# A two-layer hybrid decoder step: compression chunks, later modulation and first modulation issued in other portions

## The chip, the cores and the metric

The kernel runs on one core of one Trainium2 chip. Its time is the device time of one execution in microseconds (us), as a median of runs. The engines are named as in the profile: PE is TensorE's matrix array and PEld its weight loads, DVE is VectorE, ACT is ScalarE, POOL is GpSimd, and SP is SyncE, which here issues every DMA, in program order.

## The reference

Two layers of a trunk run over 544 tokens with D_MODEL = 1024: a prompt of 512 tokens, and 8 sequences of 4 sampled tokens with a paged past of 2048 rows each. All in float32. Per layer:

```python
mod = silu(c) @ ada_w + ada_b                 # 9 rows of c (1 prompt, 8 samples), 3072 columns
shift, scale, gate = split(mod, 3)
h = rmsnorm(x, norm_g) * (1 + scale) + shift
proj = h @ w_in                               # u, z_s5, q, k/v, gates, z_nsa, merge logits
y5 = gelu(s5_scan(u)); y5 = y5 * sigmoid(y5 @ glu_w + glu_b) * silu(z_s5)
kc, vc = compress_rows(past and new k/v)      # silu((64 rows * 64 + pe) @ w1) @ w2 per block of 64 rows
o = gated sum of compressed, selected and window attention
out = (sig(m_s5) * (y5 @ w_s5_out) + sig(m_nsa) * ((o * silu(z_nsa)) @ w_nsa_out)) @ w_o
x = x + gate * out
```

A last rmsnorm follows, and the new key/value rows, window rows and S5 states are returned too.

## The kernel before

Activations lie transposed, with features on partitions: eight blocks `k` of 128 features by 544 tokens, the tokens in two halves of 256 and 288 columns. A dense block (`wblk`, 39 per layer) is 128 output features: its 512 KB of weights are loaded, split into a high and a low part on ACT and DVE, and multiplied in 8 k-blocks x 3 matmuls x 2 halves = 48 matmuls of 128x128 weights (function `mm`).

The order of the instructions on each engine is fixed when the program is built. The code is written as threads (Python generators) with priorities, a small number first: `modulation` 4 (first) and 25 (later), `modulate` 3, compression 15, the S5 branch 2 to 6, prompt attention 20, sample attention 5, the dense stream 50. The planner `_Sched` keeps a cost model of PE, the other engines and the DMA queue, and always issues the ready thread of the smallest number; it turns to the dense stream when other work has had PE for FAIR = 12 us, or when its model of PE's load says that the present slice of time has had too few columns (`lags`). So the dense stream is the filler. Threads also wait for events (`ev`, `done`) and for columns of one arena of 49504 columns (`alloc`). Each engine then executes its list strictly in order: a matmul whose data have not landed holds back all matmuls behind it, and a DMA that waits for its buffer holds back SP's later DMAs.

What the change touches:

- `modulation` (L524) computes `mod` and `amul` = (1 + scale) * norm_g. A k-block is one 512 KB load and four matmuls of 32-column weights (`scT`) by 256 columns, side by side in four column strips of the array; they show as eight instructions, since each float32 matmul is run in two passes. Eight k-blocks give one part; per layer there are three parts, of which parts 0 and 1 hold shift and scale for four feature blocks each and part 2 the gate. The first call loads parts 0 and 1 of layer 0 (16 loads at once). The later call (`LATER`, 4 parts, 32 k-blocks) runs from event `h` of layer 0 with one buffer (`ADA_N` = 1): load, wait, four matmuls, next load.
- `modulate` (L620) makes `h`. In layer 0 it scales x by the inverse norm in place, then, for each half of the features, waits for `mod`, forms the high part on ACT, the value on DVE and the low part on DVE; the 32 sample columns go through POOL (`samples`), and their low part is a POOL subtraction (`sample_parts`).
- `first_u` (in `dense`): blocks u0 and u1 are multiplied first. With `EARLY` = 1, u0 takes the first half of the features when that half of `h` is done, and everything else follows the second half.
- `products` multiplies a compression chunk: 64 matmuls of 64-column weights by 64 columns (68 in the first chunk, 20 for the new rows), 128 instructions. It gives way after every `PROD_STEP` = 2 steps, that is after four matmuls. There are 8 chunks of past rows per layer (`compress`) and one of new rows (`compress_new`). A chunk's page rows are 16 loads of 128 KB, into one buffer in layer 0 and two in layer 1.
- `compress(1)` starts after attention of layer 0 (`att`), `s5(l)` after `h`. `ps5` and `tbank` may use PSUM bank 5 once the event `ada` says that the later modulation is done.

Of the kernel before, what the change touches and what calls it, by code (L numbers as in the profile page):

```python
# [11 lines left out]
F32 = mybir.dt.float32  # L12
# [278 lines left out]
def body(ctx: ExitStack, tc: tile.TileContext, A, O):  # L291
# [232 lines left out]
    def modulation(parts, na, pace, banks, between=None):  # L524

        n = 256
        for l, part in parts:
            if part == 0:
                L[l]["mod"] = const.tile([P, 24, 9], F32, name=nm("mod"))
                L[l]["amul"] = const.tile([P, 8, 9], F32, name=nm("amul"))  # L530
# [51 lines left out]
        done("ada", parts)  # L582

# [36 lines left out]
    def modulate(l):  # L620
# [5 lines left out]
        if l == 0:  # L626
            accb = yield from alloc(N)
            for k in range(8):
                square_acc(accb.v(N), xt(k), k)
            w_dma(1)  # L630
# [13 lines left out]
        def tokens(k, a):  # L644
            tk = evr.next().v(256)
            dve.scalar_tensor_tensor(tk, xt(k)[:, a:a + 256], amul[:, k, 0:1], rstd[:, a:a + 256],
                                     op0=ALU.mult, op1=ALU.mult)
            act.activation(hh(k, a, a + 256), tk, AF.Identity, bias=mod[:, k, 0:1])
            prev.append((hl(k, a, a + 256), tk, mod[:, k, 0:1], hh(k, a, a + 256).bitcast(F32)))
# [3 lines left out]
        def samples(ks):  # L653

            sb = [P, 4, NB, TS]
            for k2 in range(ks.start, ks.stop, 2):
                xs = xb[k2 // 2].v(2, N)[:, :, T:N]
                if l:
                    pool.tensor_tensor(ts_[:, k2:k2 + 2], xs, rstd[:, None, T:N].to_broadcast([P, 2, NS]), op=ALU.mult)
                    xs = ts_[:, k2:k2 + 2]  # L660
                xs = xs.rearrange("p k (b t) -> p k b t", t=TS)
# [4 lines left out]
        def sample_parts(ks):  # L666
            for k2 in range(ks.start, ks.stop):
                act.copy(hh(k2, T, N), ts_[:, k2])
                pool.tensor_tensor(hl(k2, T, N), ts_[:, k2], hh(k2, T, N).bitcast(F32), op=ALU.subtract)
        for half in range(2):  # L670
            if l == 0:
                ks = range(4 * half, 4 * half + 4)
                for k in ks:
                    dve.tensor_tensor(xt(k), xt(k), rstd, op=ALU.mult)
                yield t()
                w_hi(half + 1)
                w_lo(half + 1)
                yield ev("mod", l, half)
                mod, amul = q["mod"], q["amul"]
                for k in ks:  # L680
                    x_, tk = xt(k)[:, 0:T], misc.next().v(T)
                    act.activation(hh(k, 0, T), x_, AF.Identity, scale=amul[:, k, 0:1], bias=mod[:, k, 0:1])
                    dve.tensor_scalar(tk, x_, amul[:, k, 0:1], mod[:, k, 0:1], op0=ALU.mult, op1=ALU.add)
                    prev.append((hl(k, 0, T), tk, hh(k, 0, T).bitcast(F32)))
                    if len(prev) > 1:
                        dve.tensor_tensor(*prev.pop(0), op=ALU.subtract)
                dve.tensor_tensor(*prev.pop(0), op=ALU.subtract)
                done("hp", l, half)
                samples(slice(ks.start, ks.stop))
                sample_parts(ks)  # L690
            else:
                for part in range(2):
                    yield ev("mod", l, part)
                yield ev("rstd", l - 1, half)
                mod, amul = q["mod"], q["amul"]
                if half:
                    samples(slice(0, 4))
                    samples(slice(4, 8))
                for k in range(8):
                    tokens(k, 256 * half)  # L700
                    if k % 2:
                        yield t()
                dve.scalar_tensor_tensor(*prev.pop(0), op0=ALU.add, op1=ALU.subtract)
                if half:
                    sample_parts(range(8))
                done("hp", l, half)
# [9 lines left out]
    def dense(l):  # L716
# [51 lines left out]
        def first_u():  # L768
# [5 lines left out]
            if l == 0:  # L774
                outs = [[B[2 * t_ + h][:, 0:HALVES[h][1] - HALVES[h][0]] for h in range(2)] for t_ in range(2)]
                for part in range(2):
                    yield ev("hp", l, part)
                    for t_, h in ((t_, h) for t_ in range(2) for h in range(2)):
                        if t_ < EARLY:
                            yield from mm(w[t_], 0, 8, hh, hl, h, False, outs[t_][h], range(4 * part, 4 * part + 4))  # L780
                        elif part:
                            yield from mm(w[t_], 0, 8, hh, hl, h, False, outs[t_][h])
                        if part:
# [4 lines left out]
                            if t_:  # L788
                                wahead(h)
# [133 lines left out]
        def outputs():  # L923
            q["ogb"] = yield from alloc(4 * N)
# [232 lines left out]
    def ps5(l):  # L1157

        banks = ([7] if ("prs", l) in S.events else [2, 3]) + ([5] if ("ada", LATER) in S.events else [])
# [207 lines left out]
    def s5_tile(l, t_, K):  # L1367
# [8 lines left out]
        db3 = yield from alloc(1224, True)  # L1376
        yield w_
# [246 lines left out]
    def compress_new(l):  # L1624
# [5 lines left out]
        vcbd = q["vcbd"] = q["kcb"].v(8, 64, p=64, at=528)  # L1630
        cwb = []
# [682 lines left out]
```

## Time and profile before

| | |
|---|---|
| device time, median of 3 runs | 1291.28 us (1289.97 to 1294.87) |
| profiled execution: device time | 1290.52 us |
| its span, first to last instruction | 1288.7 us |
| PE / PEld busy | 1180.2 us (92%) / 1057.9 us (82%) |
| DVE / ACT / POOL busy | 781.8 us (61%) / 476.2 us (37%) / 149.2 us (12%) |
| mean granted TensorE clock | 0.959 of 2.4 GHz |
| HBM read, written | 211.84 MB, 37.98 MB |

A clock of 1.0 is 2.4 GHz, 0.5 is 1.2 GHz. The tables by stretch (windows) give the busy time of each engine in that stretch with the number of instructions that touch it, then clock, busy share of the DMA engines and GB/s. All instructions carry line 229, that of the recording helper, so operations are told apart by tile names and shapes: `scT` is modulation, weights 128x64 by 64 columns compression, weights 128x128 by 256 or 288 columns the dense stream.

### The profile page before, as it was taken

What the parts mean: (1) busy time and instruction counts of PE and PEld (TensorE: products, weight loads), DVE (VectorE), ACT (ScalarE), POOL (GpSimd) and SP (SyncE); (2) the same over time, 40 slices, a digit from 0 to 9 for tenths busy, and PEclk for the clock granted to TensorE, in tenths of its full rate; (3) what the DMA queues carried; (4) which work ended last, traced back from release to release, by engine and by line L of the source; (5) the groups of instructions that cost most, each with busy time, mean ns of one, the idle gap of its engine ahead of it and who ended that gap; (6) DMA issues with size and microseconds to landing.
All of it is one profiled execution on the core that took longest, in us unless ns stands there. A gap on an engine that the chain in (4) does not pass through costs nothing.

```text
span 1288.7 us, 30956 instructions
## 1 busy us (share of the span) xinstructions
PE 1180.2 (92%) x11994; PEld 1057.9 (82%) x11994; DVE 781.8 (61%) x1791; ACT 476.2 (37%) x1120; POOL 149.2 (12%) x337
## 2 busy tenths in 40 slices
PE   5699889989999999997998889899999999999995
PEld 2588778889887888887988878789988788789995
DVE  4575676523666676566435377876865667563744
ACT  4332332222445444443224333333444445443321
POOL 0213043100100000000001023240110000000001
PEclk9799998999999999998998999978999999999997
DMA  9576854765765767339785534545466565633742
GB/s 372 194 234 183 251 170 150 229 224 204 246 215 170 231 196 213 95 104 327 234 264 171 181 127 129 175 142 163 144 210 208 179 196 159 197 95 110 263 126 79
DMA packets 178357, 243.54 MB, mean 189 GB/s; under 512 B 33441, under 2 KB 129954, under 8 KB 176930
## 3 DMA queue, kind: packets, MB, share of 16 engines
q1 hardware_dynamic: 178210, 241.56, 59.1%
q8 instruction: 95, 1.56, 0.5%
q14 instruction: 52, 0.43, 0.1%
HBM read 211.84 MB, written 37.98 MB: 194 GB/s over the span
## 4 chain that ended last, share of the span: by engine, by line
PE 61%; DVE 13%; DMA 11%; SPq 5%; ACT 4%; issue 4%; POOL 1%; DVEq 0%; ACTq 0%
PE bank L229 61%; DVE m L229 13%; SPq L229 5%; ACT m L229 4%; DMA m<-in_ada_w 4%; DMA m<-ud 2%; DMA m<-in_cw 1%; DMA kpd<-m 1%; POOL m L229 1%; DMA m<-kpd 1%; DMA c_k<-in_k 1%; ACT L229 0%; DMA m<-in_s5k 0%; SPq L1518 0%; DMA m<-in_cmp 0%
## 5 line engine op out<-in xcount | busy, mean ns | idle before, releaser
L229 PE MATMUL bank<-m,m 128*128 128x288 f32 (+10 forms) x10796 | 1073.2, 281 | 49.3 <-DVE m L229 24.9
L229 PEld LDWEIGHTS bank<-m,m 128*128 128x128 f32 (+4 forms) x10796 | 964.5, 168 | 134.5 <-issue 48.4
L229 DVE TENSOR_TENSOR m<-m,m 128x256 f32<-128x256 f32 (+16 forms) x631 | 389.3, 640 | 175.4 <-ACT m L229 156.3
L229 ACT COPY m<-bank 128x128 f32<-128x128 f32 (+7 forms) x256 | 99.3, 398 | 341.4 <-PE bank L229 323.8
L229 ACT CAST m<-m 128x1024 fp32r<-128x1024 f32 (+6 forms) x274 | 174.5, 650 | 79.7 <-DVE m L229 47.6
L229 PE MATMUL bank<-c_k,m 128*128 128x128 f32 (+1 forms) x562 | 88.6, 285 | 18.8 <-DVE m L229 12.7
L229 ACT ACTIVATE m<-m 128x64 f32<-128x64 f32 (+7 forms) x76 | 35.4, 469 | 172.8 <-DVE m L229 163.1
L229 PEld LDWEIGHTS bank<-c_k,m 128*128 128x128 f32 (+1 forms) x562 | 65.0, 144 | 31.9 <-DVE m L229 16.5
L229 ACT ACTIVATE m<-bank 128x288 f32<-128x288 f32 (+4 forms) x130 | 50.6, 390 | 107.3 <-PE bank L229 106.8
L229 POOL TENSOR_TENSOR m<-m,m 128x32 f32<-128x32 f32 (+4 forms) x104 | 57.2, 571 | 188.8 <-ACT m L229 166.3
L229 DVE TENSOR_REDUCE m<-bank 128x1 f32<-128x384 f32 (+4 forms) x132 | 57.2, 473 | 28.8 <-PE bank L229 28.7
L229 ACT ACTIVATE m<-bank,m 128x384 f32<-128x384 f32 (+4 forms) x132 | 67.9, 524 | 18.0 <-DVE m L229 14.5
L229 POOL CAST m<-m 64x128 fp32r<-64x128 f32 x64 | 22.9, 358 | 424.1 <-ACT m L229 392.0
L229 DVE COPY m<-bank 128x32 f32<-128x32 f32 (+6 forms) x104 | 39.4, 385 | 50.1 <-ACT m L229 31.9
L229 DVE SCALAR_TENSOR_TENSOR m<-m,bank 128x256 f32<-128x256 f32 x96 | 41.3, 431 | 29.0 <-ACT m L229 13.2
L229 PE MATMUL bank<-m,scT 128*32 128x256 f32 x384 | 35.3, 463 | 24.1 <-DMA m<-in_ada_w 24.0
L229 DVE TENSOR_SCALAR m<-m,m,m 128x128 f32<-128x128 f32 (+4 forms) x132 | 52.5, 438 | 2.5
L229 POOL TENSOR_TENSOR m<-m,c_k 128x256 f32<-128x256 f32 (+2 forms) x32 | 31.3, 980 | 177.1 <-PE bank L229 145.7
L229 DVE TENSOR_TENSOR m<-bank,c_k 128x256 f32<-128x256 f32 (+5 forms) x52 | 16.7, 323 | 48.5 <-PE bank L229 47.5
L229 POOL MEMSET m<- 128x32 f32 (+5 forms) x52 | 8.3, 181 | 289.8 <-PE bank L229 149.8
L229 DVE SCALAR_TENSOR_TENSOR m<-m,m 128x64 f32<-128x64 f32 (+5 forms) x64 | 29.6, 487 | 20.1 <-ACT m L229 19.6
L229 PEld LDWEIGHTS bank<-m,scT 128*32 128x32 f32 x384 | 9.9, 123 | 33.7 <-DMA m<-in_ada_w 14.1
(62 smaller groups left out, 411.9 us busy)
## 6 DMA issues: line engine op xcount, KB each, us to landing
m<-in_wblk SPq DMA_DIRECT2D x78, 512.0 KB, 4.3
m<-in_cmp SPq DMA_DIRECT2D x256, 128.0 KB, 3.5
m<-in_kvsel SPq DMA_DIRECT2D x256, 128.0 KB, 3.1
m<-in_ada_w SPq DMA_DIRECT2D x48, 512.0 KB, 5.4
m<-in_cw SPq DMA_DIRECT2D x8, 1024.0 KB, 8.4
m<-in_wo SPq DMA_DIRECT2D x16, 512.0 KB, 3.9
ms<-m SPq DMA_DIRECT2D x16, 272.0 KB, 4.9
m<-ms SPq DMA_DIRECT2D x16, 272.0 KB, 3.7
```

Of the source, the lines that this page charges most:

```text
L229: return f(*args, **kw)
```

## The change

- First modulation in quarters: a new thread `modulation_first` (priority 2) replaces the first call. `ada_q` holds the same weights in quarters of two feature blocks, two loads of 1 MB each, all eight issued at once. A matmul takes 512 columns; the four column strips now hold four different k-blocks of the same 512 outputs, and four matmuls with a constant `fold` add the strips, where two transposes stood.
- `modulate` of layer 0 goes by quarters: per feature block two DVE operations of 512 columns with the inverse norm as an operand (the pass over x in place is gone), ACT between them; the low part of the sample columns moves from POOL to DVE. `first_u` follows in quarters with u0 and u1.
- Later modulation: the rest of layer 0 (8 k-blocks) starts after compression of layer 0, the three parts of layer 1 (24 k-blocks) after attention of layer 0. Two buffers, both k-blocks in one visit, 1.5 us of waiting added in the plan after their loads.
- `PROD_STEP` = 32: a chunk's 64 matmuls are issued in one visit.
- A new event `s5m`: `compress_new(0)` and the buffer for the outputs wait until the fourth S5 tile has its columns. `page_table` and its clamp, and the second pack of constants, are loaded after the first quarter. PSUM bank 5 is free per layer.

```diff
@@ modulation
             w = aw[i % na].v(1024)
-            yield "for", [ps], [w]
+            if i % na == 0:
+                yield "for", [ps], [b.v(1024) for b in aw]
+                yield t(ADA_LATE)
             for j in range(4):
                 pe.matmul(ps[32 * j:32 * j + 32, 0:n], scT[:, k, :], w[:, j * n:(j + 1) * n],
                           start=(k == 0), stop=(k == 7))
-            if i + na < len(todo):
-                load(i + na)
-            else:
-                aw[i % na].free()
+            if i % na == na - 1:
+                for n_ in range(na):
+                    if i + 1 + n_ < len(todo):
+                        load(i + 1 + n_)
+                    else:
+                        aw[n_].free()
@@ new
+    def modulation_first(banks):
...
+        for qd in range(4):
+            for kh in range(2):
+                sp.dma_start(aw[2 * qd + kh].v(2048), A["ada_q"][qd, kh])
+            if qd < 2:
+                w_dma(qd + 1)
+        ae = yield from alloc(512, True)
+        for qd in range(4):
+            ps, e = banks[qd % len(banks)], ae.v(512)
+            for kh in range(2):
+                w = aw[2 * qd + kh].v(4, 512)
+                yield "for", [ps], [w]
+                for j in range(4):
+                    pe.matmul(ps[32 * j:32 * j + 32, :], scT[:, 4 * kh + j, :], w[:, j, :], start=(kh == 0), stop=(kh == 1))
+                aw[2 * qd + kh].free()
+            act.copy(e, ps)
+            yield w_
+            for i in range(4):
+                pe.matmul(ps[:, 16 * i:16 * i + 9], e[:, i * P:(i + 1) * P], C["fold"][:, 0:9], start=True, stop=True)
...
+            done("modq", qd)
@@ modulate, layer 0
+        def tokens(k, a, n=256):
+            tk = misc.next().v(n) if n > 288 else evr.next().v(n)
+            dve.scalar_tensor_tensor(tk, xt(k)[:, a:a + n], amul[:, k, 0:1], rstd[:, a:a + n], op0=ALU.mult, op1=ALU.mult)
+            act.activation(hh(k, a, a + n), tk, AF.Identity, bias=mod[:, k, 0:1])
+            prev.append((hl(k, a, a + n), tk, mod[:, k, 0:1], hh(k, a, a + n).bitcast(F32)))
...
-                pool.tensor_tensor(hl(k2, T, N), ts_[:, k2], hh(k2, T, N).bitcast(F32), op=ALU.subtract)
-        for half in range(2):
-            if l == 0:
-                ks = range(4 * half, 4 * half + 4)
-                for k in ks:
-                    dve.tensor_tensor(xt(k), xt(k), rstd, op=ALU.mult)
...
+                (pool if l else dve).tensor_tensor(hl(k2, T, N), ts_[:, k2], hh(k2, T, N).bitcast(F32), op=ALU.subtract)
+        for qd in range(0 if l else 4):
+            w_hi(min(qd, 1) + 1)
+            w_lo(min(qd, 1) + 1)
+            yield ev("modq", qd)
+            mod, amul = q["mod"], q["amul"]
+            ks = slice(2 * qd, 2 * qd + 2)
+            for k in range(ks.start, ks.stop):
+                tokens(k, 0, T)
+            samples(ks)
+            dve.scalar_tensor_tensor(*prev.pop(0), op0=ALU.add, op1=ALU.subtract)
+            sample_parts(range(ks.start, ks.stop))
+            done("hp", l, qd)
@@ outputs of dense; s5_tile; compress_new
+            yield ev("s5m", l)
+        if t_ == 3:
+            done("s5m", l)
+        if l == 0:
+            yield ev("s5m", l)
@@ main
-            yield ev(*ADA_EV)
-            yield from modulation(LATER, ADA_N, ADA_PACE, [B[5]])
+            for i in range(DEPTH):
+                yield ev(*ADA_EV[i])
+                yield from modulation(LATER[i], ADA_N[i], ADA_PACE, [B[5]])
@@ constants
-LATER = ((0, 2),) + tuple((l, part) for l in range(1, DEPTH) for part in range(3))
-ADA_N = 1
+LATER = ((0, 2),), ((1, 0), (1, 1), (1, 2))
+ADA_N = 2, 2
+ADA_LATE = 1.5
-ADA_EV = 'h', 0
+ADA_EV = ('cmp', 0), ('att', 0)
-PROD_STEP = 2
+PROD_STEP = 32
```

## Rows read from the trace of the kernel before

**Rows 1.** Windows of four stretches: us, busy of each engine, clock, DMA share, GB/s.

```profile
64.00:300.00 236.00, 215.81 (x2495) 194.96 (x2493) 135.71 (x243) 65.81 (x124) 49.16 (x99) 0.96 0.68 214
...
424.00:574.00 150.00, 148.32 (x1484) 129.18 (x1483) 98.45 (x253) 68.63 (x182) 5.60 (x16) 1.00 0.54 164
574.00:604.00 30.00, 22.76 (x163) 21.12 (x162) 19.33 (x40) 10.01 (x22) 0.00 (x0) 0.92 0.85 290
...
578.00:700.00 122.00, 108.39 (x1277) 101.96 (x1276) 62.30 (x144) 36.07 (x65) 0.38 (x4) 0.94 0.80 259
```

**Rows 2.** Waits of PE for modulation weights: us, times, longest.

```profile
PE bank L229 <- DMA m<-in_ada_w: 24.0, 7, 12.4
```

**Rows 3.** Timeline of PE in the opening: start, us, instructions, idle before and releaser.

```profile
36.98 1.57 PE L229 MATMUL bank<-m,m 128*128 128x288 f32 x5 [3.16 <-POOL m L229]
...
41.23 2.27 PE L229 MATMUL bank<-m,scT 128*32 128x256 f32 x24
...
47.53 12.10 PE L229 MATMUL bank<-m,m 128*128 128x256 f32 x71 [0.51 <-DVE m L229]
63.14 0.97 PE L229 MATMUL bank<-m,scT 128*32 128x256 f32 x8 [3.52 <-DMA m<-in_ada_w]
```

**Rows 4.** Timeline of the other engines in the opening.

```profile
23.84 0.40 ACT L229 COPY m<-bank 128x288 f32<-128x288 f32 x1 [3.07 <-PE bank L229]
...
31.63 5.93 POOL L229 TENSOR_TENSOR m<-m,m 128x32 fp32r<-128x32 f32 x4 [1.76 <-ACT m L229]
...
45.34 0.20 DVE L229 SCALAR_TENSOR_TENSOR amul<-mod,c_k 128x36 f32<-128x36 f32 x1
```

**Rows 5.** Windows of two stretches of the opening's transfers.

```profile
0.00:20.00 20.00, 6.70 (x44) 3.68 (x44) 6.75 (x17) 8.49 (x13) 0.21 (x4) 1.00 0.92 349
...
23.00:29.00 6.00, 5.51 (x46) 2.45 (x48) 4.66 (x9) 2.21 (x4) 0.44 (x2) 1.00 1.05 408
```

**Rows 6.** DMA issues: count, KB each, median us from issue to landing.

```profile
m<-in_ada_w SPq DMA_DIRECT2D x48, 512.0 KB, 5.4
...
m<-in_wo SPq DMA_DIRECT2D x16, 512.0 KB, 3.9
...
m<-in_xT SPq DMA_DIRECT2D x4, 544.0 KB, 5.4
```

**Rows 7.** Groups by form: busy us, mean ns of one, of DVE's modulation in layer 1.

```profile
L229 DVE SCALAR_TENSOR_TENSOR m<-m,mod,m 128x256 fp32r<-128x256 f32 x16 | 7.9, 492 | 0.9 <-ACT m L229 0.9
L229 DVE SCALAR_TENSOR_TENSOR m<-m,amul,m 128x256 f32<-128x256 f32 x16 | 7.9, 501 | 5.4 <-ACT m L229 5.4
```

**Rows 8.** Timeline of PE at two later visits of modulation.

```profile
100.26 0.64 PE L229 MATMUL bank<-m,scT 128*32 128x256 f32 x8 [3.21 <-DMA m<-in_ada_w]
...
287.03 0.64 PE L229 MATMUL bank<-m,scT 128*32 128x256 f32 x8 [2.01 <-DMA m<-in_ada_w]
```

**Rows 9.** Windows cut at single visits on PE, start to start of the next.

```profile
73.97:75.54 1.57, 1.57 (x48) 1.50 (x48) 1.57 (x4) 0.46 (x1) 1.57 (x3) 1.00 1.01 313
...
299.26:302.90 3.64, 3.64 (x121) 3.58 (x120) 1.07 (x2) 1.47 (x2) 0.00 (x0) 1.00 0.93 349
272.62:273.00 0.38, 0.38 (x9) 0.31 (x8) 0.00 (x0) 0.00 (x0) 0.00 (x0) 1.00 0.00 0
893.30:894.90 1.60, 1.60 (x50) 1.48 (x48) 1.29 (x3) 0.28 (x1) 0.00 (x0) 1.00 0.12 37
302.90:304.53 1.63, 1.63 (x17) 1.49 (x13) 0.61 (x1) 0.00 (x0) 0.00 (x0) 1.00 0.07 28
...
652.57:661.63 9.06, 9.06 (x76) 8.93 (x72) 5.29 (x13) 3.46 (x5) 0.00 (x0) 1.00 0.81 262
84.59:85.16 0.57, 0.57 (x12) 0.16 (x9) 0.57 (x2) 0.00 (x0) 0.00 (x0) 1.00 0.00 0
```

**Rows 10.** Window of a stretch at the lower clock.

```profile
288.70:291.90 3.20, 3.20 (x16) 3.20 (x15) 0.00 (x0) 0.29 (x1) 0.00 (x0) 0.50 1.02 381
```

**Rows 11.** Timeline of ACT between the layers' attention and projection.

```profile
601.39 1.35 ACT L229 CAST m<-m 128x1024 fp32r<-128x1024 f32 x2 [7.71 <-DMA m<-in_nsaow]
```

More of the change, by code (lines that the diff above doesn't have):

```diff
@@ L527, in modulation @@
         for l, part in parts:
-            if part == 0:
+            if part == 0 and l:
                 L[l]["mod"] = const.tile([P, 24, 9], F32, name=nm("mod"))
@@ L582, in modulation @@
         done("ada", parts)
+    def modulation_first(banks):
+        mod = L[0]["mod"] = const.tile([P, 24, 9], F32, name=nm("mod"))
+        amul = L[0]["amul"] = const.tile([P, 8, 9], F32, name=nm("amul"))
+        aw = []
+        for _ in range(8):
+            aw.append((yield from alloc(2048, True)))
+        for qd in range(4):
[16 more added lines that the diff above has]
+                pe.matmul(ps[:, 16 * i:16 * i + 9], e[:, i * P:(i + 1) * P], C["fold"][:, 0:9], start=True, stop=True)
+            fs = slice(2 * qd, 2 * qd + 2)
+            src = ps[:, 0:64].rearrange("p (s q b) -> p s q b", s=2, q=2)[:, :, :, 0:9]
+            dst = mod[:, 0:16].rearrange("p (s f) b -> p s f b", s=2)[:, :, fs]
+            bia = C["ada_b"][:, 0, 0:16].rearrange("p (s f) -> p s f", s=2)[:, :, fs]
+            dve.tensor_tensor(dst, src, bia[:, :, :, None].to_broadcast([P, 2, 2, 9]), op=ALU.add)
+            dve.scalar_tensor_tensor(amul[:, fs, :], mod[:, 8 + 2 * qd:10 + 2 * qd, :], 1.0,
+                                     C["norm_g"][:, 0, fs, None].to_broadcast([P, 2, 9]), op0=ALU.add, op1=ALU.mult)
+            done("modq", qd)
+            if qd % 2:
+                done("mod", 0, qd // 2)
+            yield t()
+        ae.free()
     def rstd_of(acc, r, h):
@@ L668, in sample_parts @@
                 act.copy(hh(k2, T, N), ts_[:, k2])
-                pool.tensor_tensor(hl(k2, T, N), ts_[:, k2], hh(k2, T, N).bitcast(F32), op=ALU.subtract)
-        for half in range(2):
-            if l == 0:
-                ks = range(4 * half, 4 * half + 4)
-                for k in ks:
-                    dve.tensor_tensor(xt(k), xt(k), rstd, op=ALU.mult)
[L675 to L706, printed above, removed]
@@ new lines, in modulate @@
+        for half in range(2 if l else 0):
+            for part in range(2):
+                yield ev("mod", l, part)
+            yield ev("rstd", l - 1, half)
+            mod, amul = q["mod"], q["amul"]
+            if half:
+                samples(slice(0, 4))
+                samples(slice(4, 8))
+            for k in range(8):
+                tokens(k, 256 * half)
+                if k % 2:
+                    yield t()
+            dve.scalar_tensor_tensor(*prev.pop(0), op0=ALU.add, op1=ALU.subtract)
+            if half:
+                sample_parts(range(8))
+            done("hp", l, half)
@@ L775, in first_u @@
                 outs = [[B[2 * t_ + h][:, 0:HALVES[h][1] - HALVES[h][0]] for h in range(2)] for t_ in range(2)]
-                for part in range(2):
+                for part in range(4):
                     yield ev("hp", l, part)
[L778 to L783, printed above, removed]
+                    for t_, h in ((t_, h) for t_ in range(2) for h in range(2)) if part == 3 else ((t_, h) for h in range(2) for t_ in range(2)):
+                        if t_ and not part:
+                            continue
+                        ks = range(0 if t_ and part == 1 else 2 * part, 2 * part + 2)
+                        yield from mm(w[t_], 0, 8, hh, hl, h, False, outs[t_][h], ks)
+                        if part == 3:
                             flush()
@@ L2196, in _consts @@
     c["dmask"] = (row[:, None] % 16 == np.arange(16)[None, :]).astype(f)
+    c["fold"] = np.tile(np.eye(32, dtype=f), (4, 1))
     c["mvals"] = np.tile(np.arange(9, dtype=f), (P, 1))
```

36 lines of the change are left out of this document (14 added, 22 removed).

## Prediction

> **What bounds the kernel now.** I read the windows by stage first. From 64 to 300 us PE is busy 215.8 of 236 us, from 424 to 574 148.3 of 150, and between the two layers, from 574 to 604, only 22.8 of 30 [rows 1]. The dense stream fills PE under attention, so in these stretches a microsecond of work or of standing still that is taken from PE comes off the end, as long as nothing else becomes late. The second view is the list of waits: PE stood still for modulation weights for 24.0 us in 7 waits, 12.4 of them at the very start, when nothing can run, and 11.6 in six waits later [rows 2]. The third is PE's timeline of the opening, the fourth PE's order of instructions, cut at single visits.
>
> **The opening.** Now: PE has the first matmuls of u0 in its queue, and those that need the sample columns wait for POOL's four subtractions (5.93 us from 31.63) [rows 4]; PE stands 3.16 us at 36.98, and behind it stand the weights of the second half, which are computed only at 41.23 although they have landed [rows 3]. `amul` of that half is done at 45.5 [rows 4], u0 and u1 run from 46.4 to 59.6, then PE waits 3.52 us for the first later k-block, and u2 starts at 64 [rows 3].
>
> After: ahead of the end of the last quarter lie x (4 x 544 KB), modulation (8 MB) and two dense blocks of 512 KB [rows 6], together 11.7 MB. At 349 GB/s for 20 us and 408 after that [rows 5] it has landed at 31.5 us; I take 33 for the constants ahead of it. Behind it: one group of eight instructions of 512 columns, twice the 0.76 us that eight of 256 columns take at the mostly low clock of that place (2.27 us for 24) [rows 3], so 1.5 us; then an eviction, four small matmuls and two small DVE operations, some 2.5 us (an estimate from a 0.40 us eviction and a 0.20 us DVE operation [rows 4], with the waits between). So the last `amul` stands at 37 rather than 45.5. The inverse norm, done at 24.2 now [rows 4], is then no longer what is late. `h` of a quarter takes four DVE operations of 512 columns, each at least 0.5 us and at most twice that [rows 7], 2 to 4 us, with ACT between and the sample columns behind: the last quarter is done at 41 to 42. Its 24 matmuls take 3.0 us at 2.4 GHz (72 take 9.06 [rows 9]), 6 at 1.2. PE may still have a backlog of the 72 matmuls of the earlier quarters. So u2 starts between 45 and 53; I take 50, **-14 us** (-11 to -19). POOL and DVE have less to do here than before, and SP issues the same bytes in fewer DMAs. Moving the page table and the constants behind costs nothing: they are first used after `h`.
>
> **Waits for later weights.** After the opening five waits are left, 11.6 - 3.5 = 8.1 us [rows 2, 3], the largest 3.21 and 2.01 [rows 8]. The k-blocks leave that stretch, so **-8.1 us**; the next instruction in PE's list is dense work whose weights are loaded two blocks ahead, and SP is no longer held by buffers waiting for PE. After three of the waits (at 63, 100 and 287 us) the granted clock reads 0.50 for 3.4 us (one stretch is shown [rows 10]); at that level 3.4 us do the work of 1.7, so **-5.1 us** more. Both could be 0 if other waits take the place.
>
> **Chunks in one visit.** A visit of 8 instructions takes 0.38 us and one of 120 takes 3.64 [rows 9]: 0.029 per instruction and 0.15 to come in. Dense work pays too: 72 matmuls take 9.06 us, so 12 should take 1.51, but 12 behind a visit take 1.63 (and 1.79 elsewhere where all are of 288 columns) [rows 9]; I take 0.15, together 0.30 per visit. I count 60 visits, from 73.97 to 893.4 us (first and last in [rows 9]), over 18 chunks: 42 fewer, 12.6 us. About 20 of the 42 are in the second layer, some of them where PE has room anyway, so **-10 us** (-6 to -13). What waits behind a chunk waits up to 3.9 us (128 instructions): S5 steps, and the dense stream whose weights then are ready. The 120 instructions in a row ran at clock 1.00 [rows 9].
>
> **Two k-blocks in a visit.** 32 visits become 16. A single visit costs 0.57 us [rows 9], a k-block inside a long run 0.76 at a low clock [rows 3], so at full clock between half of that and all of it; what a visit saves is 0.15 of dense work and between -0.2 and 0.2 of its own. 16 of them: **-4 us** (+1 to -5). The PE work itself moves and stays.
>
> **What it costs.** 24 k-blocks, 12.6 MB, move into the stretch from 578 to 700 us, where the DMA engines are busy 0.80 and move 259 GB/s, 31.6 MB in 122 us [rows 1]. The added waits stand in PE's list: each of the 12 visits waits for two loads, and all dense matmuls queue behind it, and SP's loads for the next pair behind the matmuls. No row shows this traffic in this place. Lower bound 0: a load of 512 KB for the same stretch's projection lands in 3.9 us [rows 6], and the plan now adds 1.5 us of waiting. Upper bound: every visit waits as long as the longest later one did, 3.5 us [rows 3], and a low stretch of 1.7 follows it: 62 us. The nearest rows are the later visits before: 11.6 us over the 18 visits up to 287 us, 0.64 each; 12 x 0.64 = **+8 us**. At the turn itself, `nsaow` weights are already late, ACT waits 7.71 us for them [rows 11]; two more loads (1.05 MB at 340 GB/s or so) can go ahead of them: **+3 us**. The layer's `mod` is needed after 8 of the 12 visits; at 8 us for each (two loads, the 1.5 us, a place on PE) they are done 64 us after attention, some 35 us before the next layer's `h`, so that wait I put at 0. Memory: at that turn the buffers of the second modulation (2448 columns) and `h` (8976) don't both fit beside compression by my count, which would hold `h` back until the projection ends, 0 to 8 us; I take 0 since modulation should then be over. `s5m` I put at nothing: before, the fourth S5 tile had its columns long before `compress_new(0)` got its own.
>
> The page "DMA: Bandwidth & Descriptors" of the Trainium skill (Specifications) gives some 358 GB/s as the limit of one core's share of HBM. The trace passes it for a short while with 408 GB/s [rows 5]. By the page the 31.6 + 12.6 MB need at least 123 us, all of a stretch of 122; by the row 108.
>
> **Sum.** -14 - 8.1 - 5.1 - 10 - 4 + 8 + 3 = -30 us. The profiled execution took 1290.5 us (span 1288.7), so 1260; the median of the runs is 0.8 us above that execution: **1261 us**. About 0.5% (6.5 us) is what a measurement of this kernel can tell from no change.
>
> **Rivals.**
> - Part of the gain is handed back between the layers (17%). Loads crowd with page loads, the visits wait 2 us each rather than 0.64: +16, and half of the visits leave a low stretch, +10, less what is counted: -30 + 16 + 10 - 8 + 8 for `h` without columns = -4 to -12: 1279 to 1287. For it: 0.80 and 0.85 DMA shares before anything is added [rows 1]. Against it: projection loads land in 3.9 us there.
> - Slower (8%): the same place, but each of the 12 visits waits 3 us and is followed by a low stretch of 1.7: +56 + 3 - 41 = +18, 1309. It decides from (41 - 3) / 12 = 3.2 us a visit, clock included. For it: single waits of 3.5 and 3.21 have been seen [rows 3, 8]; against it, 12 of those 18 visits did not wait at all.
> - The opening doesn't get shorter (5%): at clock 0.50 the dense quarters queue up to 53 us and something else, such as the third block's weights, keeps u2 at 60: -4 instead of -14, 1271.
> - One-visit chunks lower the clock (2%): 16 chunks x 1.7 us = +27, 1288. The stretch with 120 instructions speaks against it.
> - More gain (8%): no waits at the turn and modulation filling the 7 idle us there, -41 - 7: 1242.
>
> **How the numbers follow.** The forecast, 60%, holds 1245 to 1277. Faster: 60 + 8 + 5 + two thirds of 17 (11) = 84%; within 0.5%: 6 + 2 = 8%; slower: 8%. A range from 1242 to 1285 leaves out about 6 below and 13 above.
>
> **What would show it.** Opening: the first 128x288 dense matmul of u2 near 50 us, the last `amul` near 37. Waits for `in_ada_w`: none between 64 and 300 us, new ones after 578. Compression: 18 visits of 128 instructions of 3.9 us each, and clock 1.00 behind them. Modulation's matmuls in pairs of k-blocks, 16 instructions in about 1 us. If the opening gains under 8 us, or PE's waits between 578 and 700 grow by over 25 us, the prediction is wrong.

## The result, and the profile after

The changed kernel takes **1268.5 us** (median of 4 runs, 1266.2 to 1271.5) against 1291.2 before: the ratio used here is 0.986, 95% interval 0.982 to 0.990, so about 18 us faster (13 to 23); the two medians alone divide to 0.982, the lower end of that interval. The forecast was 1261, its range 1242 to 1285. The profiled execution took 1271.5 us (span 1269.6), the longest of the four.

Most of what the prediction expected to see at single places is there. PE in the opening, and the last `amul` on DVE (it answers to [rows 3, 4]):

```profile
50.32 0.50 PE L229 MATMUL bank<-m,m 128*128 128x256 f32 x2 [0.80 <-ACT m L229]
...
41.37 0.18 DVE L229 SCALAR_TENSOR_TENSOR amul<-mod,c_k 128x18 f32<-128x18 f32 x1
```

u2 starts at 50.32 rather than 64.04, and the last `amul` is done at 41.5 (forecast 37). One visit of a chunk, as a window from its start to the start of the next matmul (it answers to [rows 9]):

```profile
264.06:267.94 3.88, 3.88 (x130) 3.81 (x129) 0.00 (x0) 0.00 (x0) 0.00 (x0) 1.00 0.91 346
```

and a visit of two k-blocks and `nsaow` on ACT in timelines (start, us, instructions, idle before and releaser):

```profile
318.84 1.07 PE L229 MATMUL bank<-m,scT 128*32 128x256 f32 x16
...
586.86 1.35 ACT L229 CAST m<-m 128x1024 fp32r<-128x1024 f32 x2 [4.87 <-DMA m<-in_nsaow]
```

There are 18 chunk visits, and PE's list of waits no longer has a row for `in_ada_w` [rows 2], not even after 578 us, where the prediction expected new ones. Between the layers `nsaow` is 4.87 us late rather than 7.71 [rows 11]. But other waits have grown. Waits of the changed kernel (us, times, longest):

```profile
PE bank L229 <- DVE m L229: 69.5, 48, 12.1
...
ACT m L229 <- DMA m<-in_wblk: 25.4, 6, 10.4
```

and the same two groups before:

```profile
PE bank L229 <- DVE m L229: 43.4, 39, 3.8
...
ACT m L229 <- DMA m<-in_wblk: 17.4, 6, 5.1
```

Part of the first growth is a change of name. PE's first instruction of all waits 12 us for its data in either kernel; before it was a modulation matmul, and the wait stood under `in_ada_w`, now it is one of the inverse norm and the wait stands under DVE. The changed kernel, then the kernel before:

```profile
12.08 1.01 PE L229 MATMUL bank<-ones,m 128*128 128x1 f32 x4 [12.08 <-DVE m L229]
```

```profile
12.40 2.24 PE L229 MATMUL bank<-m,scT 128*32 128x256 f32 x16 [12.40 <-DMA m<-in_ada_w]
```

So of the 24.0 us only 11.6 were taken away, and PE's waits for DVE grew by 14 us (43.4 to 57.5), not 26.

The windows of [rows 1] again, now of the changed kernel, and one in the first layer (length; busy us of PE, PEld, DVE, ACT, POOL with counts; granted clock, DMA share, GB/s):

```profile
64.00:300.00 236.00, 216.17 (x2636) 204.83 (x2635) 136.85 (x250) 67.13 (x130) 57.89 (x107) 0.91 0.59 179
424.00:574.00 150.00, 143.49 (x1387) 125.15 (x1386) 93.09 (x226) 66.64 (x176) 4.90 (x14) 0.98 0.52 166
574.00:604.00 30.00, 28.12 (x332) 26.13 (x330) 20.03 (x46) 9.09 (x18) 0.00 (x0) 1.00 0.96 324
578.00:700.00 122.00, 110.39 (x1512) 99.54 (x1512) 52.76 (x129) 33.73 (x59) 1.35 (x8) 0.97 0.90 300
...
276.80:293.60 16.80, 16.80 (x200) 15.16 (x198) 5.94 (x14) 2.37 (x5) 2.40 (x13) 0.50 0.43 139
```

From 64 to 300 us PE is busy as long as before, at a mean clock of 0.91 instead of 0.96; between the layers (578 to 700 us) the DMA engines move 41 GB/s more, and PE is not idle longer there. Cut where the first dense matmul of the second layer starts, the changed kernel reads:

```profile
0.00:692.20 692.20, 630.23 (x6887) 565.02 (x6887) 396.29 (x919) 247.80 (x578) 79.40 (x169) 0.95 0.65 212
692.20:1269.60 577.40, 537.06 (x5075) 492.92 (x5071) 383.68 (x875) 225.40 (x544) 80.16 (x166) 0.96 0.54 168
```

and the kernel before:

```profile
0.00:693.40 693.40, 632.16 (x6866) 554.44 (x6866) 399.47 (x921) 247.58 (x576) 75.91 (x171) 0.97 0.67 213
693.40:1288.70 595.30, 548.07 (x5131) 503.47 (x5129) 382.28 (x870) 228.64 (x545) 73.31 (x166) 0.95 0.52 161
```

This is the surprise: u2 starts 14 us earlier, and 640 us later that is 1.2 us. PE is idle 62.0 us in the first part (692.2 - 630.2) against 61.2 before.

For every kernel below I split one profiled span in the same three: PE idle; "clock loss", half of PE's busy time in stretches with a granted clock of 0.50; and the rest, PE's work at full clock. The half is an estimate: in the changed kernel two dense matmuls of 256 columns in a row start 213 ns apart at clock 0.50 and 119 at 1.00 (medians), 1.8 times and not twice. With 1.8 the clock loss of every kernel is a ninth smaller, and no difference between two rows changes by more than 3 us. "Shape changes" counts how often two matmuls in a row have weights of different shape (rows x columns). L2 is where the second layer's dense work starts.

| kernel | ratio to before (95%) | span | idle | clock loss | PE work | shape changes | L2 |
|---|---|---|---|---|---|---|---|
| before | 1 | 1288.7 | 108.5 | 43.4 | 1136.9 | 522 | 693.4 |
| changed | 0.986 (0.982 to 0.990) | 1269.6 | 102.3 | 46.9 | 1120.4 | 420 | 692.2 |
| chunks alone | 0.987 (0.982 to 0.991) | 1266.3 | 104.3 | 32.4 | 1129.7 | 458 | 696.6 |
| opening alone | 0.997 (0.994 to 1.000) | 1270.7 | 106.0 | 26.5 | 1138.2 | 530 | 690.1 |
| later modulation + `s5m` | 1.027 (1.022 to 1.031) | 1311.0 | 127.6 | 47.0 | 1136.4 | 505 | 703.0 |
| changed, small steps | 1.018 (1.014 to 1.022) | 1311.7 | 128.4 | 46.4 | 1136.9 | 500 | 726.6 |
| opening + chunks | 0.993 (0.990 to 0.996) | 1277.4 | 113.6 | 36.2 | 1127.6 | 461 | 695.0 |
| chunks + later + `s5m` | 0.992 (0.988 to 0.996) | 1278.1 | 112.0 | 45.9 | 1120.3 | 420 | 685.6 |
| changed, modulation early | 0.992 (0.988 to 0.995) | 1279.1 | 111.9 | 47.1 | 1120.2 | 417 | 697.2 |
| changed, no `s5m` | 1.014 (1.010 to 1.018) | 1295.4 | 126.6 | 45.6 | 1123.2 | 430 | 712.1 |
| `s5m` alone | 0.999 (0.996 to 1.001) | 1276.2 | 105.8 | 31.6 | 1138.8 | 524 | 691.4 |
| chunks + `s5m` | 1.002 (1.000 to 1.005) | 1282.7 | 115.6 | 40.8 | 1126.3 | 456 | 696.5 |
| opening + chunks + `s5m` | 0.996 (0.994 to 0.999) | 1272.6 | 110.2 | 35.8 | 1126.6 | 455 | 687.3 |
| changed, small steps in layer 2 | 1.015 (1.013 to 1.018) | 1288.9 | 120.7 | 42.8 | 1125.5 | 434 | 705.1 |

Ratios are compared, not times: beside the experiments the kernel before had medians of 1282.7 to 1284.3 us. A span is one execution; that of small steps in layer 2 was the shortest of its five (1293.2 us, median 1301.2), that of the opening alone the shortest of its twelve.

### The profile page after: what moved, and what is told of

Same layout as the page of the kernel before. It is cut to its first block, busy times and chain, and to the rows that moved or that the text cites. A ratio compares the mean times of both kernels' runs of the same rounds, so it can differ in the third digit from the quotient of the medians.

```text
span 1269.6 us, 30887 instructions
## 1 busy us (share of the span) xinstructions
PE 1167.3 (92%) x11958; PEld 1057.9 (83%) x11958; DVE 780.0 (61%) x1793; ACT 473.2 (37%) x1122; POOL 159.6 (13%) x335
## 4 chain that ended last, share of the span: by engine, by line
PE 57%; DVE 16%; DMA 13%; SPq 5%; ACT 4%; issue 3%; DVEq 0%; ACTq 0%
PE bank L229 57%; DVE m L229 16%; SPq L229 4%; ACT m L229 3%; DMA m<-in_wblk 2%; DMA m<-in_wo 2%; DMA m<-kpd 1%; DMA m<-in_cmp 1%; DMA m<-in_xT 1%; DMA yd<-m 1%; DMA m<-in_cw 1%; DMA kpd<-m 1%; DMA x_mid<-m 1%; DMA m<-mn 0%; DMA ms<-m 0%
## 5 line engine op out<-in xcount | busy, mean ns | idle before, releaser
L229 PE MATMUL bank<-m,m 128*128 128x288 f32 (+11 forms) x10796 | 1069.2, 282 | 48.7 <-DVE m L229 30.0
L229 DVE TENSOR_TENSOR m<-m,m 128x256 f32<-128x256 f32 (+15 forms) x623 | 382.6, 636 | 163.4 <-ACT m L229 139.6
L229 ACT CAST m<-m 128x1024 fp32r<-128x1024 f32 (+7 forms) x274 | 174.9, 650 | 97.8 <-DVE m L229 57.0
L229 ACT ACTIVATE m<-m 128x64 f32<-128x64 f32 (+6 forms) x76 | 35.2, 469 | 172.9 <-DVE m L229 164.9
L229 PEld LDWEIGHTS bank<-c_k,m 128*128 128x128 f32 x590 | 67.8, 145 | 34.2 <-DVE m L229 25.3
L229 ACT ACTIVATE m<-bank 128x256 f32<-128x256 f32 (+3 forms) x130 | 49.9, 389 | 88.4 <-PE bank L229 83.7
L229 DVE TENSOR_REDUCE m<-bank 128x1 f32<-128x128 f32 (+4 forms) x132 | 57.2, 473 | 16.6 <-PE bank L229 16.1
L229 DVE SCALAR_TENSOR_TENSOR m<-m,bank 128x256 f32<-128x256 f32 x96 | 41.4, 433 | 32.6 <-PE bank L229 13.3
L229 DVE SCALAR_TENSOR_TENSOR m<-m,m 128x256 f32<-128x256 f32 (+5 forms) x64 | 28.3, 466 | 45.1 <-ACT m L229 44.6
L229 DVE SCALAR_TENSOR_TENSOR m<-bank,mod,m 128x256 f32<-128x256 f32 x32 | 15.2, 480 | 40.7 <-PE bank L229 28.3
L229 ACT ACTIVATE m<-m,m 128x512 f32<-128x512 f32 (+2 forms) x24 | 15.9, 662 | 58.9 <-DVE m L229 53.8
```

Of the source, the lines that this page charges most:

```text
L229: return f(*args, **kw)
```

## Experiments

**Each part alone, and the change without its chunks.**

```diff
# chunks alone: before, with
-PROD_STEP = 2
+PROD_STEP = 32
```

> The kernel before with one edit: all products of a compression chunk in one visit. By the prediction's sum (0.30 us for each of 42 visits saved, some of it where PE has room): -10 us against before, 1281, with 18 runs of 128 instructions of 3.9 us in PE's list. Rival (a run of small matmuls lowers the granted clock, or dense weights become late behind it): the visits are saved in the list, but half-clock stretches appear that are not there before, and the time stays within 3 us of before, 1288 to 1294.

Measured 0.987, some 17 us less: more than the prediction's 10. PE work fell by 7.2, clock loss by 11, idle by 4. The rival is wrong: no more of the lower clock than before. The whole gain of the change, from one constant. What the visits themselves cost is only the 7.2; no run says why the rest goes, and clock loss differs by 10 us between executions of one list of instructions, as shown further down.

```diff
# opening alone: changed, with the rest as before
-PROD_STEP = 32
+PROD_STEP = 2
-LATER = ((0, 2),), ((1, 0), (1, 1), (1, 2))
-ADA_N = 2, 2
-ADA_EV = ('cmp', 0), ('att', 0)
+LATER = ((0, 2),) + tuple((l, part) for l in range(1, DEPTH) for part in range(3))
+ADA_N = 1
+ADA_EV = 'h', 0
...
-            yield ev("s5m", l)
-                yield t(ADA_LATE)
```

> The kernel before with the new opening alone (first modulation in quarters, u0 and u1 in quarters, inverse norm inside the token step); chunks and later modulation as before. By the prediction's sum: -14 us, 1277, the first matmul of u2 near 50 us rather than 64. By the profile of the changed kernel, whose opening is the same, also -14 at u2; the rival is that the later modulation, which starts at the same event and is now 14 us ahead, waits for its weights as before or more, and gives 3 to 6 us of it back: 1280 to 1283.

Measured 0.997: 4 us, not 14, and not because of `in_ada_w` as the rival had it (PE waits 7.5 us in 5 for it). By the profiles the gain is lost under attention. From the end of the compression of new tokens to the first page load of the next compression, this kernel and the kernel before:

```profile
321.30:584.00 262.70, 244.82 (x2380) 208.78 (x2381) 174.28 (x471) 118.79 (x338) 12.69 (x36) 0.99 0.56 171
```

```profile
312.30:588.00 275.70, 270.25 (x2661) 232.48 (x2660) 180.75 (x479) 127.54 (x356) 15.08 (x45) 1.00 0.60 184
```

and PE's main wait in the same two windows, in that order:

```profile
PE bank L229 <- DVE m L229: 13.6, 15, 2.1
```

```profile
PE bank L229 <- DVE m L229: 3.6, 9, 1.1
```

Attention starts 9 us later here, not earlier: the compression of new tokens, which comes ahead of it, loads its weights at 296.8 us instead of 285.3, 1 us behind the fourth S5 tile (295.7 instead of 232.0). PE did dense work meanwhile: 1308 dense matmuls of the first layer are done at the start of this stretch, against 1092. Being 216 matmuls ahead, the kernel puts fewer of them between attention's steps (972 against 1163); PE waits 12 us more, and at the end of attention it is only 25 ahead (488 left, 513 before). That the missing matmuls cause the waits is an argument: over the fourteen kernels the number done at attention's start and PE's idle time under it go together only loosely (correlation 0.5).

```diff
# later modulation + s5m: before, with
-LATER = ((0, 2),) + tuple((l, part) for l in range(1, DEPTH) for part in range(3))
-ADA_N = 1
-ADA_EV = 'h', 0
+LATER = ((0, 2),), ((1, 0), (1, 1), (1, 2))
+ADA_N = 2, 2
+ADA_EV = ('cmp', 0), ('att', 0)
...
+            yield ev("s5m", l)
+                yield t(ADA_LATE)
```

> The kernel before with the later modulation alone moved: gate of the first layer behind compression, the second layer's behind attention, two k-blocks in a visit, and the two waits that put the fourth S5 tile ahead. By the prediction's sum -8.1 (waits) -5.1 (clock) -4 (visits) +8 (turn) +3 (nsaow) = -6 us, 1285. Theory from the two traces: the waits that go are replaced by others between 262 and 322 us (dense weights behind the two 1 MB loads of the compression of new tokens, the start of attention), and nothing is left: 1289 to 1294. Rival on the other side: the turn between the layers costs more than the 6 us of idle time seen there, 1296 or more.

Measured 1.027, 34 us slower: the rival on the other side. From the last dense matmul of the first layer to the 720th of the second, this kernel and the changed one:

```profile
688.80:878.10 189.30, 160.12 (x1570) 145.94 (x1568) 136.04 (x271) 62.07 (x129) 52.23 (x101) 0.89 0.50 157
```

```profile
682.10:843.80 161.70, 146.16 (x1524) 135.16 (x1523) 117.83 (x243) 58.00 (x123) 46.50 (x88) 0.96 0.59 182
```

PE is idle 29.2 us in it against 15.5, only 2.0 of them for `in_ada_w`: what is late is not the modulation's weights. The last experiment shows a part of it.

```diff
# changed, small steps
-PROD_STEP = 32
+PROD_STEP = 2
```

> The changed kernel with one edit undone: the products of a compression chunk in small steps again, the opening and the later modulation as changed. If the one visit is worth 10 us as predicted: 1278 against 1268 of the changed kernel. If it costs through the clock what it saves in visits: within 3 us of the changed kernel, with 42 visits more in PE's list and fewer half-clock stretches between 120 and 300 us (25 us of them in the changed kernel).

Measured 1.018: taking the one visit away costs 3.2%, some 41 us, four times what the larger of the two theories said. Only 16.5 of it are PE work (the span is 42 longer); 26 are PE idle.

**Pairs, another place for modulation, and the `s5m` waits.**

```diff
# opening + chunks: the opening alone, with
-PROD_STEP = 2
+PROD_STEP = 32
# chunks + later + s5m: later modulation + s5m, with
-PROD_STEP = 2
+PROD_STEP = 32
# changed, modulation early: changed, with (and bank 5 lent out only after LATER[-1])
-ADA_EV = ('cmp', 0), ('att', 0)
+ADA_EV = ('cmp', 0), ('cmp', 0)
# changed, no s5m
-            yield ev("s5m", l)
```

> The changed kernel without its later modulation: the new opening and the chunks in one visit, modulation of the gate and of the second layer in single k-blocks from `h` on as before, no wait for the fourth S5 tile. If moving the modulation is what costs time between the layers (from the last dense matmul of the first layer to the 720th of the second 165 to 168 us without it, 189 to 191 with it, in the runs with small steps), this is faster than the changed kernel: about 1256, ratio to before 0.977 to 0.981. Rival: only small steps and the moved modulation together are bad, with one-visit chunks the move is worth what the prediction said (-6 us): this is 6 us slower than the changed kernel, ratio 0.990 or more.

Measured 0.993: the rival. With one-visit chunks the moved modulation, together with its waits, is no loss, and the opening on top of the chunks gains nothing (0.993 against 0.987).

> The changed kernel without its opening: one-visit chunks and the moved modulation alone. If the move costs some 10 us at the turn with one-visit chunks too: slower than chunks alone, ratio to before 0.993 to 1.0 (chunks alone: 0.987). If the opening is what gives nothing (0.997 alone) and the move is neutral: 0.987.

Measured 0.992, at the edge of the first theory's span: a little slower than chunks alone, though PE work is 9.4 us less (1120.3 against 1129.7). What the pairs save there, idle (+7.7) and clock (+13.5) give back.

> The changed kernel with the second layer's modulation starting behind compression of the first layer, as the gate's does, rather than behind its attention (and the spare bank given to others only when that modulation is over). If the 12 visits at the turn are what costs: the stretch from the last dense matmul of the first layer to the 720th of the second is 10 us shorter than the changed kernel's 161.7 us, the time 5 to 12 us less than the changed kernel's. Rival (the turn is bound by page loads and the S5 chain, not by the visits): no difference of more than 3 us.

Measured 0.992, on the slower side; the stretch meant was 159.9 us rather than 161.7. The passage between the layers is not bound by the visits. With them under attention that stretch is longer instead (315 us from the compression of new tokens to the next page load, 270 in the changed kernel), with 117 more dense matmuls in it.

> The changed kernel without its two waits for the fourth S5 tile's columns (ahead of the compression of new tokens and of the attention output's buffer). If these waits hold attention up (dense work for q, k and v is done at 197.5 us, the compression of new tokens starts at 282): that compression starts 10 to 20 us earlier and the time falls by up to 10 us. The prediction put them at nothing: then it starts at 275 to 285 and the time is within 3 us.

Measured 1.014: the two waits that the prediction put at nothing are worth 2.8% here, and the theory had the sign wrong. Beside opening + chunks (0.993) it says more: without the waits the moved modulation costs 2.1%, though the chunks are in one visit. Without them the compression of new tokens comes later, not earlier. Its weights (`in_cw`) on SP, in this kernel and in the changed one:

```profile
283.79 4.46 SPq L229 DMA_DIRECT2D m<-in_cw  x2
```

```profile
262.69 0.81 SPq L229 DMA_DIRECT2D m<-in_cw  x2
```

Attention ends 25 us later (584.3 against 559.5), and with it begins all that waits for its end, modulation too. PE meanwhile ran dense work ahead (1224 matmuls rather than 1080 when attention starts) and idles more under attention (23.1 us against 10.8). That the buffer of attention's output takes the columns first is what the code suggests; no run shows it.

**The waits without the modulation.**

```diff
# s5m alone: before, with
+            yield ev("s5m", l)
...
+        if t_ == 3:
+            done("s5m", l)
...
+        if l == 0:
+            yield ev("s5m", l)
# chunks + s5m; opening + chunks + s5m: the same lines
```

> The kernel before with the two waits for the fourth S5 tile's columns alone (the attention output's buffer and, in the first layer, the compression of new tokens come behind that tile). They decide who gets memory first and move no work of their own. The prediction put them at nothing: within 5 us of before, ratio 0.996 to 1.004; then the 2.7% that the later modulation cost with these waits is the modulation's. Theory from the runs so far (what counts is when the fourth S5 tile and the compression of new tokens get their columns): the fourth tile's load comes 5 to 10 us earlier than 232 us, the compression of new tokens ends 10 to 20 us earlier than 312 us, and the time falls by 5 to 15 us, 0.988 to 0.996. Rival: the waits with small compression steps are what makes it slower: ratio 1.02 or more.

> Chunks in one visit and the two waits for the fourth S5 tile's columns; opening and modulation as before. Theory (memory order): the fourth tile's load, at 257 us with chunks alone, comes before 240; compression of new tokens ends before 281; the time is that of chunks alone or up to 10 us less, ratio 0.978 to 0.987. If the waits only help where opening and modulation are changed: 0.987 to 0.995, not better than chunks alone.

> The changed kernel with its modulation of the gate and the second layer as before (single k-blocks from `h` on), all else as changed. Without the two waits this was 0.993. If the waits are worth here what they are worth in the changed kernel (1.014 without, 0.986 with): 0.970 to 0.980, better than the changed kernel, and the moved modulation is a loss. If the moved modulation and the waits only work together (the modulation's buffers no longer taking the columns that the fourth tile needs): 0.990 or more.

Measured 0.999, 1.002 and 0.996. Alone the waits change nothing that can be told apart, as the prediction had it. On top of chunks they cost 1.6%; my memory theory, which wanted a gain there, fails in that form. And against the last of the three the changed kernel's moved modulation is worth 1.0%: 13 us, more than the 6 forecast, but only with one-visit chunks and the waits together.

**Where the chunks and the modulation meet.**

```diff
# changed, small steps in layer 2
-PROD_STEP = 32
+PROD_STEP = 32, 2          # by layer
```

> The changed kernel with small compression steps in the second layer alone (its eight chunks between the layers and its compression of new tokens); the first layer keeps its chunks in one visit. With small steps in both layers the profiled span was 42 us longer than the changed kernel's: 20 of them up to the last dense matmul of the first layer, 22 behind it. If the loss sits where the chunks are (each layer its own): this is 18 to 25 us above the changed kernel, ratio to before 1.000 to 1.006, with the last dense matmul of the first layer at 680 to 690 us and the stretch from there to the 720th of the second at 185 us or more. If the first layer's chunks cause all of it (they put attention back, and the turn follows): within 5 us of the changed kernel, 0.984 to 0.990. Third: only more PE work, 8 chunks x 2.3 more visits x 0.3 us, 6 us, 0.991.

Measured 1.015: the loss sits where the chunks are, and is larger than expected. The last dense matmul of the first layer came earlier than expected, at 670.2 us, and the stretch from there to the 720th of the second took 195.1. PE's list is the changed kernel's up to the first of these chunks, so the place is seen alone. Between the last dense matmul of the first layer and the first of the second, this kernel and the changed one:

```profile
670.20:705.10 34.90, 21.92 (x487) 17.27 (x486) 7.52 (x26) 5.17 (x13) 3.28 (x9) 0.82 0.51 167
```

```profile
682.10:692.20 10.10, 6.80 (x159) 5.74 (x157) 5.01 (x16) 1.88 (x6) 0.00 (x0) 1.00 0.88 300
```

PE, DVE, POOL and SP in the long one (timelines):

```profile
673.67 0.63 DVE L229 TENSOR_SCALAR m<-c_k,rsc 128x128 f32<-128x128 f32 x3
...
675.45 0.69 PE L229 MATMUL bank<-m,m 128*64 128x64 f32 x16
676.17 7.39 SPq L229 DMA_DIRECT2D m<-in_cmp  x12
...
680.40 1.07 PE L229 MATMUL bank<-m,scT 128*32 128x256 f32 x16
692.12 5.58 PE L229 MATMUL bank<-m,m 128*64 128x64 f32 x128 [10.65 <-DMA m<-in_cmp]
697.63 1.07 PE L229 MATMUL bank<-m,scT 128*32 128x256 f32 x16
...
703.24 0.20 DVE L229 SCALAR_TENSOR_TENSOR amul<-mod,c_k 128x36 f32<-128x36 f32 x1
703.35 0.92 DVE L229 SCALAR_TENSOR_TENSOR m<-m,amul,m 128x256 f32<-128x256 f32 x2
703.58 0.41 POOL L229 TENSOR_TENSOR m<-m,amul 128x64 f32<-128x64 f32 x1 [25.37 <-DVE amul L229]
...
705.12 3.19 PE L229 MATMUL bank<-m,m 128*128 128x256 f32 x12
```

and the changed kernel, with the inverse norm on ACT (first half) and DVE (second half) beside the same two DVE instructions:

```profile
681.87 0.36 ACT L229 COPY m<-bank 128x256 f32<-128x256 f32 x1
...
683.46 0.20 DVE L229 SCALAR_TENSOR_TENSOR amul<-mod,c_k 128x36 f32<-128x36 f32 x1
...
689.85 0.62 DVE L229 TENSOR_SCALAR m<-c_k,rsc 128x128 f32<-128x128 f32 x3
...
690.39 0.86 DVE L229 SCALAR_TENSOR_TENSOR m<-m,amul,m 128x256 f32<-128x256 f32 x2
```

The inverse norm that the second layer's `h` needs passes its last DVE operation at 674 us; ACT writes out its first half at 668.2 and its second at 676.0. `h` (the last DVE row) begins at 703.35, right behind the last `amul`: it waited 27 us for the layer's **modulation**, and POOL's row names the same wait, 25.37 us for `amul`. The eighth of modulation's visits, which that `amul` needs, stands in PE's list behind a chunk, and the chunk behind its pages for 10.65 us. These pages are late through the small steps too: their buffer came free when an earlier chunk ended on PE, at 676.14; SP, which waited 3.3 us for it, issues them from 676.17. In the changed kernel `amul` is done 7 us before `h` begins. That is no margin in the data: the first half of the inverse norm was there at 682.2, 1.4 us before `amul`, and `h` begins at 690.39 because in DVE's list it stands behind the second half's inverse norm. All kernels whose second modulation was moved, sorted by ratio (attention's end is the first page load of the next compression):

| kernel | ratio | attention's end | visits 1 to 8 (apart) | last `amul` | `h` begins |
|---|---|---|---|---|---|
| changed | 0.986 | 559.5 | 581.9 to 673.9 (13.1) | 683.5 | 690.4 |
| changed, modulation early | 0.992 | 605.5 | ahead of attention's end | 457.7 | 694.6 |
| chunks + later + `s5m` | 0.992 | 557.6 | 563.6 to 653.6 (12.9) | 668.1 | 676.8 |
| changed, no `s5m` | 1.014 | 584.3 | 601.6 to 698.4 (13.8) | 710.9 | 711.0 |
| changed, small steps in layer 2 | 1.015 | 548.2 | 570.6 to 697.6 (18.1) | 703.2 | 703.4 |
| changed, small steps | 1.018 | 591.7 | 595.3 to 723.0 (18.2) | 725.5 | 725.6 |
| later modulation + `s5m` | 1.027 | 559.4 | 572.9 to 699.4 (18.1) | 701.8 | 701.9 |

The four slow kernels are the four in which `h` begins within 0.2 us of the last `amul`. A chunk has priority 15, modulation 25: in small steps a chunk holds PE for 7.5 to 9.6 us for most of the eight and modulation's visits come 18 us apart, in one visit 4.0 us and 13 apart.

The late `h` is a part of the loss, not all of it. From the second half of the inverse norm to `h` the four kernels, in the order of the table, wait 12, 27, 16 and 7 us, while their spans are 26, 19, 42 and 41 us longer than the changed kernel's: the one that waits least loses nearly the most. PE's idle time between the last dense matmul of the first layer and the first of the second is 8.1, 13.0, 9.2 and 2.5 us (3.3 in the changed kernel), of 18 to 26 us that they idle more in all. With small steps in layer 2 another 12 us of it come between there and the 720th dense matmul, where PE mostly waits for DVE; without `s5m` 14 us lie ahead of attention's end; with later modulation + `s5m` 16 us of the loss are PE work and 14 us idle time behind the first dense matmul of the second layer. The direct test, small steps with the second layer's modulation early, was not run. No version that was run is faster than the changed kernel beyond its interval; chunks alone equals it.

## Why the prediction was right, and where it was not

**The time**: 1268.5 lies in the range, 7.5 above the forecast and inside the main case (1245 to 1277), not in the rival that hands part of the gain back (1279 to 1287). The mechanism was half right. Of the -30 us forecast the ratio shows -18, nearly all of it PE's work, and the terms on waits gave next to nothing. That the whole is a gain at all is in part luck: the three parts, each alone, multiply to a loss.

**Terms on PE's work came.** Chunks -10 and pairs -4 were forecast; the profiled spans show -16.5 (1136.9 to 1120.4), which is nearly the whole gain of 18. Over the fourteen kernels a straight line through PE work and shape changes gives an estimate of 0.167 us for each change (correlation 0.98, every kernel within 2.3 us of it); a visit has two, 0.33 us, and the prediction took 0.30. The Trainium skill, "TensorEngine Tiling (Array Packing)", section Key Properties, says that a change of tiling mode drains the engine. The rows agree in that each change costs time; that the cost is a drain no run here shows.

**Terms on waits did not come.** -14, -8.1, -5.1, +8 and +3 are together -16.2 us of idle and clock; these two went from 151.9 to 149.2. The step that failed is the first paragraph's: "a microsecond of work or of standing still that is taken from PE comes off the end, as long as nothing else becomes late". Something else did become late: PE's idle time is 102.3 us against 108.5, and its clock loss 46.9 against 43.4.
- *Opening -14*: u2 came at 50.3, as forecast (the last `amul` at 41.4 rather than 37). What follows it was not forecast: alone 4 us, on top of chunks a loss of 0.7% (the two intervals touch), on the other three bases a gain of 0.6 to 0.8%. By the prediction's own sign, "if the opening gains under 8 us", it was wrong here: 14 us at u2, but 4 in the time. Attention's start does not follow u2. What it follows is not shown: `in_cw` is issued 1 to 3 us behind the fourth S5 tile's load in opening alone, chunks alone and opening + chunks, and 12 to 57 us behind it in the others.
- *Waits for weights -8.1, clock -5.1*: the waits are gone, and `in_wblk` behind two 1 MB loads of `in_cw` (ACT waits 10.44 us at 273.55) and DVE at the start of attention (PE 4.62 us at 309.11) stand there instead, with the 16.8 us at clock 0.50 shown above.
- *Passage between the layers +8, `nsaow` +3*: not seen. DMA moved 300 GB/s and PE's idle time there did not grow.
- *`h` behind modulation 0*: "at 8 us for each ... they are done 64 us after attention, some 35 us before the next layer's `h`". The visits came 13.1 us apart and the last `amul` 124 us after attention's end, 7 us before `h`. The value 0 held, but not by the 35 us: by the data there was no margin left, and where the visits come further apart (small steps) or attention ends later, `h` waits for them, 27 us in the kernel with small steps in layer 2.
- *`s5m` 0*: right alone (0.999), wrong by 2.8% inside the change, where without these waits the moved modulation is a loss of 2.1% instead of a gain of 1.0%.
- *The sum itself*: the three parts alone multiply to 0.987 x 0.997 x 1.027 = 1.010; together they are 0.986. Some 31 us belong to no part. The later modulation alone did what the slower rival said, in part at its place (28 of its 41 us over the changed kernel come between the last dense matmul of the first layer and the 720th of the second), and not by its mechanism: PE waits 2.0 us there for `in_ada_w`. `h` waiting for visits that stand behind chunks is a part of it.

What stays open: why the `s5m` waits cost the kernel with chunks alone 1.6%; why chunks alone gain 10 us more than their PE work; and where the slow kernels lose what `h`'s wait does not explain. And clock loss is no sure reading from one profile: the kernel with small steps in layer 2 runs the changed kernel's PE list up to attention's end, and got there at 548.2 us rather than 559.5, with nearly the same idle time (47.0 and 49.1 us) but 17.3 us of clock loss instead of 27.4.

## What to carry to other kernels

Count work saved on the full engine at its price; count a wait removed at nothing until you have shown what the stream that fills the gaps does instead; here it ran ahead, and the time was lost again later. When work moves to a place with a due time, measure how far apart its steps come behind work of higher priority there, and what its margin is. Parts that share memory and an issue order are measured together and apart: here their effects differ in sign.

## What was not expected of the hardware

The lower clock differs from run to run for the same list of instructions by 10 us up to 560 us, as above; over 21 runs of the kernel before the mean granted clock lay between 0.959 and 0.968 and the time between 1277.7 and 1291.4 us, the longer times mostly at the lower clocks (correlation -0.75). By the line through the fourteen kernels PE pays 0.167 us for each change of the shape of the weights; for 417 to 530 changes that is an estimate of 70 to 89 us of a span.
